# First products taken on x * g with rstd applied later, first loads in order of use on one queue, and w_ada loads moved to that queue

## The chip, the cores and the metric

The kernel runs on one core of one Trainium2 chip. The metric is the device time of one execution in microseconds (us), lower is better. The engines are TensorE (PE; PEld is its weight load), VectorE (DVE), ScalarE (ACT), GpSimd (POOL) and SyncE (SP). Each takes its instructions in order; SP does nothing here but issue DMAs.

## The reference

Two transformer blocks on 256 tokens of width 2048, in float32. What matters here is the beginning of the first block, and the context path and the modulation vectors of the second:

```python
def rms_norm(x, g):
    y = xf * lax.rsqrt(jnp.mean(xf * xf, axis=-1, keepdims=True) + NORM_EPS)
    return (y * g).astype(x.dtype)
def first_block(...):
    h = rms_norm(x, pre_mix_g[l])
    z = h @ w_in[l]                       # q, k, v for chunked attention, u for a pooling branch
    ...
def adaln(cond, w_ada, b_ada):
    return jnp.split(jax.nn.silu(cond) @ w_ada + b_ada, ADA_CHUNKS, axis=-1)
def second_block(...):
    m_lat = [m[:, None, :] for m in adaln(c, w_ada[l], b_ada[l])]
    m_ctx = adaln(c_ctx, w_ada[l], b_ada[l])
    hc = modulate(rms_norm_2(ctx, norm1_g[l]), m_ctx[0], m_ctx[1])
    pc = hc @ w_in_l[:, :KV_WIDTH]
    ...
```

The first block ends with an up and a down projection with a convolution between them (ffn1); the second projects K and V of context and tokens (w2kv), queries and gates, attends, merges (wbr, wout) and has a feed-forward layer of its own.

## The kernel before

All large weights stream through one ring (`Stream`). A *piece* is 128 x 1024 values, 512 KB, loaded by SP into one of four buffers w (L204). `prep` makes of it a rounded part h (ScalarE, L237) and the rest l (VectorE, L238), five buffers each; it may run four pieces ahead of TensorE. A piece is two *slabs* of 512 columns. A slab is used by `token_major` (tokens by outputs, three products per tile: L392, L393, L395) or `feature_major` (outputs by tokens, L359, emptied by `folded`, L367 and L368). After each slab `done` prepares what it can, and adds `pace` to a credit; each full credit runs one `step`.

A step is one product of the modulation (L536): VectorE multiplies a 128 x 1024 tile v of w_ada with a row of the condition that lies broadcast in SBUF (`crow`, L510), and sums it. The tiles, 192 in all, are loaded by GpSimd into two buffers v (L211), each reissued by the step that has read it. The first 64 tiles serve two steps each, the others one. `PACE` holds the steps per slab for feature-major and token-major work; `limit` says up to which tile the steps may go in a stage.

```python
PACE = ((0.2, 0.3), (0.24, 0.36), None, (0.0, 0.3), (0.1, 0.13))   # block1, ffn1, -, wbr and wout, last layer
self.pace = 0.0, (132 - S.vdone) / 80                             # K and V of block 2, at tile 88
```

The limits are 64 and then 88 tiles up to the end of ffn1, 128 in K and V of block 2, 160 in wbr and wout, and 192. In K and V of block 2 a slab is used for four token tiles, and a chunk of 16 slabs fills four of seven PSUM banks, which are emptied at its end.

`Side` holds tasks as Python generators; `tick`, once a slab, lets them emit their next part, and a yield of n waits n ticks. So the order of the instructions on each engine is the order in which this code runs. One such task is `ctx_norm`. It starts in ffn1 when the modulation of the context is known, and goes twice through a tile of the context: it loads each of four parts of 512 columns and squares it (L883, ScalarE L477), forms rstd (L428, and a power on GpSimd, L429), loads each part again (L890), scales it (VectorE, L892), transposes it on TensorE (L452), applies the modulation (L459, L461) and splits it into h and l (L337, L338). The loads go to a ring of two buffers and are issued by GpSimd, as are the w_ada loads.

At the start, x is loaded in pieces of 512 columns, tile 0, then the gain, then weights, then tile 1. Each tile's squares are summed, rstd is formed, x is scaled by rstd and gain (L439), transposed and split. `staged` runs the first eight blocks of 128 inputs for tile 0 alone, then tile 1 is made ready, and the other blocks follow. The result of this first product is half of v; q, k and u follow feature-major.

Of the kernel before, what the change touches and what calls it, by code (L numbers as in the profile page):

```python
# [190 lines left out]
class Stream:  # L191
# [4 lines left out]
    def __init__(self, nc, w, h, l, v, side):  # L196
        self.nc, self.w, self.h, self.l, self.v, self.side = nc, w, h, l, v, side
        self.items, self.vitems, self.steps = [], [], deque()
        self.loaded = self.mains = self.pos = self.retired = self.vloaded = self.vdone = 0
        self.pace, self.credit, self.limit, self.hold = 0.0, 0.0, 0, 0  # L200

    def load(self):
        while self.loaded < len(self.items) and self.loaded < self.mains + len(self.w):
            self.nc.sync.dma_start(self.w[self.loaded % len(self.w)], self.items[self.loaded])  # L204
            self.loaded += 1

    def vload(self):
        while self.vloaded < len(self.vitems) and self.vloaded < self.vdone + len(self.v):
            src, fns = self.vitems[self.vloaded]
            t = self.v[self.vloaded % len(self.v)]  # L210
            self.nc.gpsimd.dma_start(t, src)  # L211
            self.vloaded += 1
            for k, fn in enumerate(fns):
                self.steps.append((fn, t, k == len(fns) - 1))

    def step(self):
        if not self.steps:
            self.vload()
        fn, t, last = self.steps.popleft()
        fn(t)  # L220
        if last:
            self.vdone += 1
            self.vload()

    def finish(self):
        while self.vdone < self.limit:
# [30 lines left out]
    def done(self, ahead=True):  # L257

        self.pos += 1
        self.retired = self.pos // 2  # L260
        if not ahead:
            return
        self.fill()
        self.credit += self.pace
        while self.credit >= 1:
            self.credit -= 1
            if self.vdone < self.limit and self.side.now >= self.hold:
                self.step()


class Kernel:
# [200 lines left out]
    def norm_t(self, *args):  # L472
        for step in self.norm_b(*args):
            step()
# [13 lines left out]
    def constants(self):  # L488
        nc, a = self.nc, self.a
        self.ident = self.g(P)  # L490
        self.ones = self.g(2)
        self.mhalf = self.g(1)
        self.vecs = self.g(NVEC)
        self.ada_v = {n: self.g(16) for n in ("sh1", "sc1", "csh1", "csc1", "sh2", "sc2", "gate")}
        self.g1, self.gc1, self.g2 = self.g(16), self.g(16), self.g(16)
        self.lam, self.ss = self.g(1), self.g(8)
        self.subln = self.g(1)
        self.stats = self.g(128)
        self.sti = 0
        self.junk = self.g(512)  # L500
        self.small = self.g(P)
# [97 lines left out]
    def block1(self):  # L599
        nc, a, side, S = self.nc, self.a, self.side, self.S  # L600
        side.limit, side.per = 1, 1

        xt = self.slot(6, F32).rearrange("p (t d) -> p t d", t=2)
        hx, hh, hl = self.pair(0)
        xr = a["x"].rearrange("(t p) d -> p t d", p=P)
        nc.scalar.copy(self.stats[:, 0:1], self.mhalf)
        grow = self.slot(4, F32)[:, :D]
        for t in range(2):
            for c in range(4):
                nc.sync.dma_start(xt[:, t, c * 512:(c + 1) * 512], xr[:, t, c * 512:(c + 1) * 512])  # L610
            if t == 0:
                nc.sync.dma_start(grow, a["prg"].to_broadcast([P, D]))
                S.load()
        nc.scalar.dma_start(self.vecs, a["vec"])
        self.xs = self.ring(512, 4)

        def start(t):
            ss = self.stat(4)
            for c in range(4):
                self.sumsq(xt[:, t, c * 512:(c + 1) * 512], ss[:, c:c + 1])  # L620
            return self.pre_norm(t, xt, ss, grow)
        self.meet(self.norm_b(start(0), 0, hh, hl))
        xs1 = start(1)
        first = self.token_major([(hh, hl, 0), (hh, hl, 1)], self.staged(lambda: self.norm_t(xs1, 1, hh, hl)))

        _, ah, al = self.pair(2)
        qk = self.slot(4, F32R).rearrange("p (s k t) -> p s k t", s=4, k=4)
# [5 lines left out]
        scr = [s6[:, 2048 + i * 384:2048 + (i + 1) * 384] for i in range(4)]  # L633
        self.gtop = self.gbase + 1024 + 2048
        ut = self.g(8 * 272).rearrange("p (k t) -> p k t", k=8)
        pa, pb = (self.g(544).rearrange("p (k t) -> p k t", k=2) for _ in range(2))
# [57 lines left out]

        def uproj():
            for fb in range(8):
                self.folded(self.feature_major(hx), ut[:, fb, 16:])
                if fb % 2:
                    side.add(pool(fb // 2))

        def qkproj(which):
            z = None
            for j in range(5):
                last, z = z, self.folded(self.feature_major(hx), xq[j % 2]) if j < 4 else None
                if j:
                    self.split(qk[:, 2 * which, j - 1, :], qk[:, 2 * which + 1, j - 1, :], last)

        def mix():
# [19 lines left out]
        def head(h):  # L728

            j = h % 4  # L730
# [3 lines left out]
            bank = self.sb()  # L734
# [4 lines left out]
            sc = 1.0 / math.sqrt(P)  # L739
            mx, sm = self.stat(2), self.stat(2)  # L740
            for q, (lo, hi) in enumerate(((0, P), (P, 384))):
                nc.vector.scalar_tensor_tensor(s[:, lo:hi], bank[:, 2 * lo:2 * lo + hi - lo], sc, tab[:, h, P:] if q == 0 else tab[:, h, :],
                                               op0=ALU.mult, op1=ALU.add)
                nc.vector.reduce_max(mx[:, q:q + 1], s[:, lo:hi], axis=AX, negate=True)
                nc.scalar.activation(s[:, lo:hi], s[:, lo:hi], AF.Exp, bias=mx[:, q:q + 1], accum_out=sm[:, q:q + 1])
# [7 lines left out]
            bank = self.sb()  # L753
# [9 lines left out]
            bank = self.sb()  # L763
# [829 lines left out]
```

## Time and profile before

| | before |
|---|---|
| median of 3 runs | 2799.04 us (2794.86 to 2801.4) |
| the profiled execution | 2798.22 us, span 2796.1 us |
| TensorE busy | 2709.5 us |
| VectorE busy | 2017.0 us |
| ScalarE busy | 1335.9 us |
| GpSimd busy | 254.0 us |

The span runs from the first to the last instruction of the profiled execution; some 2 us of its time lie around it. Busy time leaves out DMA issues and waits. The granted clock, 1 for 2.4 GHz and 0.5 for 1.2 GHz, has a mean of 0.989 over the span.

### The profile page before, as it was taken

The page shows a single profiled execution, that of the slowest core. Times are in us where ns is not written, and L with a number is a line of the kernel's source. Part 1 is how long each engine was busy: PE and PEld are TensorE (multiplying, and loading weights), DVE is VectorE, ACT ScalarE, POOL GpSimd, SP SyncE. Part 2 cuts the span into 40 slices and gives each one's busy share as a digit, 9 for nine tenths or more (in the row PEclk, how much of TensorE's full clock was granted, in tenths as well). Part 3 has the DMA queues.
Part 4 walks back from the last instruction along what each step waited for, and adds up shares of the span by engine and source line. Part 5 has one row for each costly group of instructions (what it writes and reads, how often), then busy time and mean ns, then how long its engine had stood idle before and what let it go on. Part 6 is the DMA issues. An engine that isn't in the chain of part 4 may idle for free.

```text
span 2796.1 us, 36791 instructions
## 1 busy us (share of the span) xinstructions
PE 2709.5 (97%) x13654; PEld 2281.2 (82%) x13654; DVE 2017.0 (72%) x2938; ACT 1335.9 (48%) x1994; POOL 254.0 (9%) x397
## 2 busy tenths in 40 slices
PE   8999899999998799999999999999999999999999
PEld 6888787888877688787877788888878888888887
DVE  6888787888877676746567777768766666665566
ACT  5544454545453455522256665544454444444443
POOL 1121000000001100213111010011100000000000
PEclk9999999999998899999999999999999999999999
DMA  7577567676767675565755544489847776766565
GB/s 283 188 235 270 188 211 256 222 257 227 264 223 249 211 234 171 188 231 177 247 188 173 175 163 153 143 302 327 296 162 235 229 234 227 236 205 190 189 201 168
DMA packets 167860, 609.95 MB, mean 218 GB/s; under 512 B 19504, under 2 KB 19696, under 8 KB 166656
## 3 DMA queue, kind: packets, MB, share of 16 engines
q1 hardware_dynamic: 127728, 461.43, 49.1%
q0 software_dynamic: 39808, 145.92, 15.8%
q8 instruction: 107, 1.75, 0.3%
q14 instruction: 73, 0.60, 0.1%
q10 hardware_dynamic: 144, 0.25, 0.0%
HBM read 592.81 MB, written 14.71 MB: 217 GB/s over the span
## 4 chain that ended last, share of the span: by engine, by line
PE 74%; DVE 6%; issue 4%; ACT 3%; DMA 2%; POOL 1%; ACTq 0%; DVEq 0%; POOLq 0%
PE bank L359 29%; PE bank L392 14%; PE bank L393 14%; PE bank L395 14%; DVE l L238 2%; DMA G<-ctx 1%; ACT h L237 1%; DVE G L536 1%; PE bank L342 1%; PE bank L343 1%; PE bank L344 1%; PE bank L1288 1%; PE bank L452 0%; ACT G L477 0%; ACT G L459 0%
## 5 line engine op out<-in xcount | busy, mean ns | idle before, releaser
L238 DVE TENSOR_TENSOR l<-w,h 128x1024 fp32r<-128x1024 f32 x870 | 1063.0, 1228 | 429.8 <-ACT h L237 418.9
L237 ACT CAST h<-w 128x1024 fp32r<-128x1024 f32 x870 | 908.4, 1051 | 591.8 <-PE bank L393 408.7
L359 PE MATMUL bank<-pair,h 128*128 128x512 f32 x3072 | 847.6, 397 | 11.8 <-ACT h L237 11.8
L359 PEld LDWEIGHTS bank<-pair,h 128*128 128x128 f32 x3072 | 529.4, 190 | 82.4 <-ACT h L237 12.6
L392 PE MATMUL bank<-h,pair 128*128 128x512 f32 x1344 | 535.4, 398 | 11.3 <-DVE slot L1203 5.9
L393 PE MATMUL bank<-h,pair 128*128 128x512 f32 x1344 | 526.9, 392 | 1.4 <-DVE pair L338 0.7
L359 PEld LDWEIGHTS bank<-pair,l 128*128 128x128 f32 x3072 | 472.6, 189 | 66.9 <-DVE l L238 0.4
L359 PE MATMUL bank<-pair,l 128*128 128x256 f32 x3072 | 489.9, 281 | 0.0
L395 PE MATMUL bank<-l,pair 128*128 128x512 f32 x1344 | 413.4, 393 | 6.0 <-DVE l L238 5.9
L536 DVE CUSTOM_DVE_ANT_0 G<-v,G 128x1024 bf16<-128x1024 f32 x256 | 329.3, 1286 | 23.6 <-DMA v<-wada 22.6
L392 PE MATMUL bank<-h,slot 128*128 128x512 f32 x768 | 303.2, 395 | 10.6 <-ACT slot L337 7.2
L392 PEld LDWEIGHTS bank<-h,pair 128*128 128x128 f32 x1344 | 253.9, 189 | 69.6 <-issue 12.9
L395 PEld LDWEIGHTS bank<-l,pair 128*128 128x128 f32 x1344 | 254.0, 189 | 63.1 <-DVE l L238 9.0
L393 PE MATMUL bank<-h,slot 128*128 128x512 f32 x768 | 302.5, 394 | 2.0 <-DVE slot L338 2.0
L393 PEld LDWEIGHTS bank<-h,pair 128*128 128x128 f32 x1344 | 253.9, 189 | 52.8 <-DVE pair L338 2.7
L395 PE MATMUL bank<-l,slot 128*128 128x512 f32 x768 | 240.3, 393 | 0.0
L211 POOL DMA_DIRECT2D v<-wada x192 | 102.1, 532 | 1424.2 <-DVE G L536 1371.2
L367 ACT COPY G<-bank 128x256 f32<-128x256 f32 x192 | 71.4, 372 | 263.9 <-PE bank L359 263.9
L392 PEld LDWEIGHTS bank<-h,slot 128*128 128x128 f32 x768 | 146.3, 191 | 42.2 <-ACT slot L337 8.5
L393 PEld LDWEIGHTS bank<-h,slot 128*128 128x128 f32 x768 | 146.3, 191 | 33.9 <-DVE slot L338 3.4
L395 PEld LDWEIGHTS bank<-l,slot 128*128 128x128 f32 x768 | 145.8, 190 | 30.7
L368 DVE TENSOR_TENSOR G<-bank,G 128x256 f32<-128x256 f32 x192 | 81.1, 422 | 121.9 <-ACT G L367 121.7
(217 smaller groups left out, 1710.0 us busy)
## 6 DMA issues: line engine op xcount, KB each, us to landing
v<-wada POOLq DMA_DIRECT2D x192, 512.0 KB, 4.9
w<-wup SPq DMA_DIRECT2D x176, 512.0 KB, 4.4
w<-wgu SPq DMA_DIRECT2D x176, 512.0 KB, 4.0
w<-wdn SPq DMA_DIRECT2D x88, 512.0 KB, 4.5
w<-wfd SPq DMA_DIRECT2D x88, 512.0 KB, 4.0
w<-w SPq DMA_DIRECT2D x66, 512.0 KB, 4.3
w<-w2g SPq DMA_DIRECT2D x64, 512.0 KB, 3.6
w<-w2kv SPq DMA_DIRECT2D x52, 512.0 KB, 4.2
```

What stands on the lines that cost most here:

```text
L211: self.nc.gpsimd.dma_start(t, src)
L237: self.nc.scalar.copy(h, w)
L238: self.nc.vector.tensor_sub(l, w, h.bitcast(F32))
L342: t.matmul(out, ah, bh, start=start, stop=False)
L343: t.matmul(out, ah, bl, start=False, stop=False)
L359: t.matmul(bank[:, :size], w[:, j * P:(j + 1) * P], x[:, kb, :size], start=s == n == 0, stop=s == 3 and n == 7)
L367: self.nc.scalar.copy(z, bank[:, 256:])
L368: self.nc.vector.tensor_add(out, bank[:, :256], z)
L392: self.nc.tensor.matmul(banks[i], xh, h, start=seen[i] == 1, stop=False)
L393: self.nc.tensor.matmul(banks[i], xl, h, start=False, stop=False)
L395: self.nc.tensor.matmul(banks[i], xh, l, start=False, stop=seen[i] == total[i])
L536: nc.vector.tensor_tensor_reduce(out=self.junk.bitcast(mybir.dt.bfloat16), in0=w, in1=self.adat[:, slot * 1024:(slot + 1) * 1024], scale=1 ...
```

## The change

Three things. First, the first products are taken on x * g: rstd, which is one number per token, is applied to the results. v is multiplied as it leaves PSUM (ScalarE with a scale, VectorE with a scalar), u and k by a row of rstd that goes to DRAM and comes back to all partitions (`rt`), and q through the factor on the scores (`rq`). Second, x, gain and the first weights are loaded by SP in pieces in the order of their use, and the first product takes its 16 blocks once for both tiles, with the products, transposes and splits of the next four blocks emitted between them. Third, w_ada is loaded by SP, and the load that refills a buffer is no longer issued by the step that read it, but by `done` when a count (`vdue`, set to 2 by each step) has run out.

```diff
@@ Stream
-    def load(self):
-        while self.loaded < len(self.items) and self.loaded < self.mains + len(self.w):
+    def load(self, most=None):
+        most = len(self.items) if most is None else most
+        while self.loaded < most and self.loaded < self.mains + len(self.w):
...
-            self.nc.gpsimd.dma_start(t, src)
+            self.nc.sync.dma_start(t, src)
...
         if last:
             self.vdone += 1
-            self.vload()
+            self.vdue = 2
...
         self.fill()
+        self.vdue -= 1
+        if self.vdue == 0:
+            self.vload()
         self.credit += self.pace
...
@@ ada_begin
         self.S.limit, self.S.hold = limit, self.side.now + ROWS
+        if not self.S.steps:
+            self.S.vload()
@@ block1
+        for c in range(4):
+            nc.sync.dma_start(xt[:, 0, cs[c]], xr[:, 0, cs[c]])
+            nc.sync.dma_start(grow[:, cs[c]], a["prg"][:, cs[c]].to_broadcast([P, 512]))
+            if c < 2:
+                S.load(2 * c + 1)
+            nc.sync.dma_start(xt[:, 1, cs[c]], xr[:, 1, cs[c]])
+            if c < 2:
+                S.load(2 * c + 2)
...
+        def scaled(c, t):
+            z, bank = xs(), self.sb()
+            nc.vector.tensor_mul(z, xt[:, t, cs[c]], grow[:, cs[c]])
+            for j in range(4):
+                nc.tensor.transpose(bank[:, j * P:(j + 1) * P], z[:, j * P:(j + 1) * P], self.ident)
+            return bank
...
+        def chunk(c):
+            for t, bank in enumerate([scaled(c, 0), scaled(c, 1)]):
+                parts(c, t, bank)
+                S.prep()
+            squares(c - 1)
...
+        first = self.token_major([(hh, hl, 0), (hh, hl, 1)], [
+            self.seg(range(1), ahead=False, after=lambda: chunk(1)), self.seg(range(1, 5), ahead=False, after=lambda: chunk(2)),
+            self.seg(range(5, 9), ahead=False, after=lambda: chunk(3)), self.seg(range(9, 12), after=lambda: squares(3)),
+            self.seg(range(12, KB))])
+        rrow = self.dpool.tile([1, 256], F32, name="rrow")
         for t in range(2):
...
+            self.rstd(ss[t], D, rr[:, t:t + 1], count=4)
+            nc.gpsimd.dma_start(rrow[:, t * P:(t + 1) * P].rearrange("o p -> p o"), rr[:, t:t + 1])
+        nc.vector.tensor_scalar_mul(rq, rr, 1.0 / math.sqrt(P))
...
+        nc.gpsimd.dma_start(rt, rrow.to_broadcast([P, 256]))
...
-                self.folded(self.feature_major(hx), ut[:, fb, 16:])
+                u = self.folded(self.feature_major(hx), ut[:, fb, 16:])
+                nc.vector.tensor_mul(u, u, rt)
...
+                    if which:
+                        nc.vector.tensor_mul(last, last, rt)
...
-                self.split(vt[:, 0, t, :], vt[:, 1, t, :], banks[t])
+                v, r = vt[:, 0, t, :], rr[:, t:t + 1]
+                nc.scalar.activation(v, banks[t], AF.Identity, scale=r)
+                nc.vector.scalar_tensor_tensor(vt[:, 1, t, :], banks[t], r, v.bitcast(F32), op0=ALU.mult, op1=ALU.subtract)
```

The change shifts later lines: L211, L238, L338, L429, L439 become L212, L239, L342, L433 and L630, and L883, L890 and L510 become L926, L933 and L514. The order of the instructions moves at three places. A row names line, operation, output and input; in brackets stand the engines and DMA counters that it waits for.

GpSimd before, in the stretch of `ctx_norm`, from the broadcasts of the condition to the third load for scaling (L429 is the power of rstd):

```order
L510 DMA G<-crow 128x1024 [waits DVE_49] x2
L211 DMA v_93<-wada 128x1024 [waits DMASW6_49]
L883 DMA G<-ctx 128x512 x2
L883 DMA G<-ctx 128x512 [waits DMASW3_49,Activation_49]
L211 DMA v_92<-wada 128x1024 [waits DMASW7_49,DVE_49]
L883 DMA G<-ctx 128x512 [waits DMASW4_49,Activation_49]
L211 DMA v_93<-wada 128x1024 [waits DMASW2_49,DMASW0_49,DVE_49]
L429 TENSOR_TENSOR G<-G 128x1 [waits DVE_49]
L890 DMA G<-ctx 128x512 [waits DMASW5_49,DMASW1_49,Activation_49]
...
L890 DMA G<-ctx 128x512 [waits DMASW7_49,Activation_49]
...
L890 DMA G<-ctx 128x512 [waits Activation_49]
```

The same place of GpSimd in the change:

```order
L514 DMA G<-crow 128x1024 [waits DMASW3_49,DMASW1_49,DVE_49]
L926 DMA G<-ctx 128x512 [waits DMASW6_49,DMASW4_49]
L926 DMA G<-ctx 128x512 [waits DMASW7_49,DMASW5_49]
L926 DMA G<-ctx 128x512 [waits DMASW4_49,Activation_49]
L926 DMA G<-ctx 128x512 [waits DMASW5_49,Activation_49]
L433 TENSOR_TENSOR G<-G 128x1 [waits DVE_49]
L933 DMA G<-ctx 128x512 [waits DMASW6_49,Activation_49]
L933 DMA G<-ctx 128x512 [waits DMASW7_49,Activation_49]
L933 DMA G<-ctx 128x512 [waits DMASW2_49,DVE_49]
L933 DMA G<-ctx 128x512 [waits DMASW3_49,DVE_49]
```

Between the loads of ctx stood the issues of w_ada, seven of them between the first and the third load for scaling; now nothing stands there but the power. The wait for VectorE of the third and fourth scaling load is that for its own buffer.

SP in the change, in the down projection at the same time, where before only the rows of w stood:

```order
L205 DMA w_80<-wdn 128x1024 [waits DMAHW5_49,DVE_49]
L212 DMA v_93<-wada 128x1024 [waits DMAHW3_49]
L205 DMA w_81<-wdn 128x1024 [waits DMAHW6_49,DVE_49]
L212 DMA v_92<-wada 128x1024 [waits DMAHW0_49]
L205 DMA w_78<-wdn 128x1024 [waits DMAHW7_49,DVE_49]
L205 DMA w_79<-wdn 128x1024 [waits DMAHW1_49,DVE_49]
L212 DMA v_93<-wada 128x1024 [waits DMAHW3_49]
```

The w_ada loads stand behind weight loads that wait for VectorE, and have no wait of their own for it, here and in all 192 rows.

VectorE before, at the start of the program (L426 and L428 form rstd, l_87 is the l part of the first piece, pair_105 holds the split rows):

```order
L426 TENSOR_REDUCE G<-G 128x1 [waits Activation_49]
L428 TENSOR_SCALAR G<-G 128x1 [waits DVE_49]
L439 SCALAR_TENSOR_TENSOR G<-slot_104,G,slot_107 128x512 [waits DMAHW4_49,DMAHW0_49,Pool_49]
L439 SCALAR_TENSOR_TENSOR G<-slot_104,G,slot_107 128x512 [waits DMAHW1_49]
L439 SCALAR_TENSOR_TENSOR G<-slot_104,G,slot_107 128x512 [waits DMAHW2_49]
L439 SCALAR_TENSOR_TENSOR G<-slot_104,G,slot_107 128x512 [waits DMAHW3_49]
L238 TENSOR_TENSOR l_87<-w_78,h_82 128x1024 [waits DMAHW5_49,Activation_49]
L338 TENSOR_TENSOR pair_105<-bank_75,pair_105 128x4x128 [waits Activation_49]
```

VectorE in the change, at the same place:

```order
L630 TENSOR_TENSOR G<-slot_104,slot_106 128x512 [waits DMAHW2_49,DMAHW1_49]
L239 TENSOR_TENSOR l_87<-w_78,h_82 128x1024 [waits DMAHW3_49,Activation_49]
L342 TENSOR_TENSOR pair_105<-bank_75,pair_105 128x4x128 [waits Activation_49]
L630 TENSOR_TENSOR G<-slot_104,slot_106 128x512 [waits DMAHW4_49]
L239 TENSOR_TENSOR l_88<-w_79,h_83 128x1024 [waits DMAHW5_49,Activation_49]
L342 TENSOR_TENSOR pair_105<-bank_76,pair_105 128x4x128 [waits Activation_49]
L630 TENSOR_TENSOR G<-slot_104,slot_106 128x512 [waits DMAHW7_49,DMAHW6_49]
L630 TENSOR_TENSOR G<-slot_104,slot_106 128x512 [waits DMAHW1_49]
```

The first product of x no longer follows a chain through squares and rstd, and waits only for two loads; the second one, of tile 1, stands behind the first l part and the first split.

## Rows read from the trace of the kernel before

**Rows 1.** Busy time of an engine over the whole span, from the page.

```profile
PE 2709.5 (97%) x13654; PEld 2281.2 (82%) x13654; DVE 2017.0 (72%) x2938; ACT 1335.9 (48%) x1994; POOL 254.0 (9%) x397
```

**Rows 2.** Busy time by stretch: its length, PE, PEld, DVE, ACT, POOL, clock, DMA share.

```profile
140.00:205.00 65.00, 63.21 (x346) 54.48 (x344) 57.57 (x79) 31.26 (x46) 13.87 (x12) 1.00 0.70 234
...
820.00:893.00 73.00, 59.61 (x248) 47.87 (x247) 53.27 (x81) 26.46 (x37) 10.12 (x19) 0.89 0.74 255
893.00:975.00 82.00, 63.63 (x317) 54.18 (x316) 52.38 (x85) 35.98 (x66) 9.26 (x17) 0.87 0.58 195
...
1180.00:1325.00 145.00, 140.72 (x606) 115.58 (x606) 87.21 (x129) 32.70 (x38) 35.49 (x48) 0.98 0.58 198
...
1830.00:2050.00 220.00, 218.91 (x993) 180.86 (x991) 162.56 (x199) 89.46 (x104) 24.32 (x46) 1.00 0.81 291
```

**Rows 3.** TensorE's waits: us in total, times, longest.

```profile
PE bank L452 <- DVE G L892: 12.5, 4, 5.0
PE bank L359 <- ACT h L237: 11.8, 3, 5.9
```

**Rows 4.** Waits of the other engines from 820 to 975 us.

```profile
POOL v L211 <- DVE G L536: 110.9, 19, 13.3
ACT G L477 <- DMA G<-ctx: 32.3, 5, 7.8
...
DVE G L892 <- DMA G<-ctx: 11.8, 3, 4.7
```

**Rows 5.** Timeline near 870 us: start, length; in brackets the idle time before and its end.

```profile
849.62 0.69 DVE L338 TENSOR_TENSOR pair<-G,pair 128x512 fp32r<-128x512 f32 x1 [0.69 <-ACT pair L337]
...
865.15 0.53 POOL L211 DMA_DIRECT2D v<-wada  x1 [3.81 <-DVE G L536]
865.67 0.54 POOL L890 DMA_DIRECT2D G<-ctx  x1
...
872.91 0.49 DVE L892 TENSOR_SCALAR G<-G 128x512 f32<-128x512 f32 x1 [4.55 <-DMA G<-ctx]
...
873.45 0.71 PE L452 MATMUL bank<-G 128*128 128x128 f32 x4 [1.94 <-DVE G L892]
```

**Rows 6.** Timeline of the start, up to the first feature-major matmul.

```profile
4.31 0.63 ACT L477 ACTIVATE G<-slot 128x512 f32<-128x512 f32 x1 [2.09 <-DMA slot<-x]
...
8.69 0.57 POOL L429 TENSOR_TENSOR G<-G 128x1 f32<-128x1 f32 x1 [7.30 <-DVE G L428]
9.84 2.74 DVE L439 SCALAR_TENSOR_TENSOR G<-slot,G,slot 128x512 f32<-128x512 f32 x4 [1.30 <-DMA slot<-prg]
...
11.00 1.05 ACT L237 CAST h<-w 128x1024 fp32r<-128x1024 f32 x1 [2.85 <-DMA w<-w]
...
13.87 0.48 PE L392 MATMUL bank<-h,pair 128*128 128x512 f32 x1
...
39.04 0.39 PE L392 MATMUL bank<-h,pair 128*128 128x512 f32 x1
...
40.40 1.07 PE L359 MATMUL bank<-pair,h 128*128 128x512 f32 x4
```

**Rows 7.** DMA issues: count, KB each, median us to landing; whole span, then stretches.

```profile
v<-wada POOLq DMA_DIRECT2D x192, 512.0 KB, 4.9
w<-wup SPq DMA_DIRECT2D x176, 512.0 KB, 4.4
...
v<-wada POOLq DMA_DIRECT2D x25, 512.0 KB, 4.7
...
w<-wbr SPq DMA_DIRECT2D x46, 512.0 KB, 5.4
...
crow<-G POOLq DMA_DIRECT2D x1, 16.0 KB, 3.3
```

**Rows 8.** Groups of instructions: busy us, mean ns of one, idle before.

```profile
L238 DVE TENSOR_TENSOR l<-w,h 128x1024 fp32r<-128x1024 f32 x870 | 1063.0, 1228 | 429.8 <-ACT h L237 418.9
...
L368 DVE TENSOR_TENSOR G<-bank,G 128x256 f32<-128x256 f32 x192 | 81.1, 422 | 121.9 <-ACT G L367 121.7
```

More of the change, by code (lines that the diff above doesn't have):

```diff
@@ L199, in __init__ @@
         self.loaded = self.mains = self.pos = self.retired = self.vloaded = self.vdone = 0
-        self.pace, self.credit, self.limit, self.hold = 0.0, 0.0, 0, 0
-    def load(self):
-        while self.loaded < len(self.items) and self.loaded < self.mains + len(self.w):
+        self.pace, self.credit, self.limit, self.hold, self.vdue = 0.0, 0.0, 0, 0, 0
+    def load(self, most=None):
+        most = len(self.items) if most is None else most
+        while self.loaded < most and self.loaded < self.mains + len(self.w):
             self.nc.sync.dma_start(self.w[self.loaded % len(self.w)], self.items[self.loaded])
@@ L500, in constants @@
         self.junk = self.g(512)
-        self.small = self.g(P)
+        self.small, self.rx = self.g(P), self.g(4)
         make_identity(nc, self.ident)
@@ L605, in block1 @@
         xr = a["x"].rearrange("(t p) d -> p t d", p=P)
-        nc.scalar.copy(self.stats[:, 0:1], self.mhalf)
-        grow = self.slot(4, F32)[:, :D]
-        for t in range(2):
[L609 to L624, printed above, removed]
+        grow = self.slot(4, F32)[:, :D]
+        cs = [slice(c * 512, (c + 1) * 512) for c in range(4)]
@@ new lines, in block1 @@
+        for c in range(4):
[6 more added lines that the diff above has]
+                S.load(2 * c + 2)
+        nc.scalar.dma_start(self.vecs, a["vec"])
+        nc.scalar.copy(self.stats[:, 0:1], self.mhalf)
+        xs = self.ring(512, 4)
@@ new lines, in block1, with parts @@
+        ss = [self.ss[:, :4], self.ss[:, 4:]]
+        rq, rr = self.rx[:, :2], self.rx[:, 2:]
+        def scaled(c, t):
[4 more added lines that the diff above has]
+            return bank
+        def parts(c, t, bank):
+            self.split(*(d[:, 4 * c:4 * c + 4, t * P:(t + 1) * P] for d in (hh, hl)), bank.rearrange("p (k t) -> p k t", k=4))
@@ new lines, in chunk, with squares @@
+        def chunk(c):
[3 more added lines that the diff above has]
+            squares(c - 1)
+        def squares(c):
+            for t in range(2):
+                self.sumsq(xt[:, t, cs[c]], ss[t][:, c:c + 1])
+        begin = [scaled(0, 0)]
+        S.prep()
+        parts(0, 0, begin[0])
+        begin.append(scaled(0, 1))
+        S.prep()
+        parts(0, 1, begin[1])
+        first = self.token_major([(hh, hl, 0), (hh, hl, 1)], [
+            self.seg(range(1), ahead=False, after=lambda: chunk(1)), self.seg(range(1, 5), ahead=False, after=lambda: chunk(2)),
+            self.seg(range(5, 9), ahead=False, after=lambda: chunk(3)), self.seg(range(9, 12), after=lambda: squares(3)),
+            self.seg(range(12, KB))])
@@ L633, in block1 @@
         scr = [s6[:, 2048 + i * 384:2048 + (i + 1) * 384] for i in range(4)]
+        rt = s6[:, 3584:3840]
+        nc.gpsimd.dma_start(rt, rrow.to_broadcast([P, 256]))
         self.gtop = self.gbase + 1024 + 2048
@@ L738, in head @@
             s = scr[j]
-            sc = 1.0 / math.sqrt(P)
             mx, sm = self.stat(2), self.stat(2)
             for q, (lo, hi) in enumerate(((0, P), (P, 384))):
-                nc.vector.scalar_tensor_tensor(s[:, lo:hi], bank[:, 2 * lo:2 * lo + hi - lo], sc, tab[:, h, P:] if q == 0 else tab[:, h, :],
+                nc.vector.scalar_tensor_tensor(s[:, lo:hi], bank[:, 2 * lo:2 * lo + hi - lo], rq[:, q:q + 1], tab[:, h, P:] if q == 0 else tab[:, h, :],
                                                op0=ALU.mult, op1=ALU.add)
```

## The prediction

> **What bounds the kernel now.** I read the busy table first: TensorE is busy for 97% of the span [rows 1], so a change elsewhere can only win what TensorE spends idle or at the lower of its two clock levels. The table of stretches shows where that time lies. From 820 to 975 us TensorE is busy for 59.6 of 73 and 63.6 of 82 us, and the mean granted clock is 0.89 and 0.87 [rows 2]; in the other stretches shown it is busy for 97 to 99.5%. The list of TensorE's waits names the cause's last link: in that stretch it waits 12.5 us for the scaled context rows and 11.8 us for a cast of weights [rows 3]. The waits of the other engines give the link before: ScalarE waits 32.3 us there for loads of ctx to square, VectorE 11.8 us for loads of ctx to scale, and GpSimd spends 110.9 us waiting to issue w_ada loads [rows 4].
>
> The timeline shows how these hang together [rows 5]. The buffer that a ctx load fills was free at 850.3 us, when VectorE's split had read it (849.62 + 0.69). But GpSimd issues in order, and ahead of this load stood four w_ada loads, each waiting until VectorE has read its buffer; the last of them went out at 865.15. So the ctx load went out at 865.67, landed at 872.9, VectorE had sat idle for 4.55 us by then, and TensorE, whose transposes come next in its order, for 1.94. Meanwhile the l parts of later weights stood behind the same VectorE instruction. The pattern repeats for most of the ctx loads.
>
> The other idle time is the start: first main matmul at 13.87 us, first feature-major matmul, which ends the first product, at 40.40 [rows 6].
>
> **The ctx stretch, the largest term.** All 192 w_ada issues leave GpSimd. The ctx loads keep their program order, but now wait only for their own buffers: for the third scaling load that is the split at 850.3, some 15 us earlier than 865.67. A landing of 7.2 us (865.67 to 872.9) is then over by 858, and VectorE came to its scaling near 868 (872.91 less 4.55). The first squares' load stays late: it is issued after the broadcasts of the condition vector, as before. What can be won is TensorE's idle time, 13.4 + 18.4 = 31.8 us, and the clock: a mean of 0.89 and 0.87 between levels of 1 and 0.5 (2.4 and 1.2 GHz) puts 0.22 x 73 + 0.26 x 82 = 37.4 us at the lower one; TensorE was busy for 123.2 of 155 us, so about half of 0.795 x 37.4, that is 14.9 us, is lost. Together 46.7 us: TensorE's own work there is 108 us.
>
> VectorE won't let it have all of this. It works 53.3 + 52.4 = 105.7 us in the stretch [rows 2], almost as long. To that come the bubbles where it waits for ScalarE's half of a split (0.69 us in rows 5, for eight context chunks 5.5 us), and new waits for w_ada: the reload now goes out two slabs after the read, so that in the part with 11 loads at 0.36 a slab the lead falls from 5 or 6 slabs to 3 or 4, that is 4.1 to 5.4 us at 1.36 a slab (40.40 - 39.04 [rows 6]), against a landing of 4.9 [rows 7]: 0 to 0.8 us each, at most 9. VectorE then needs 111 to 120 us. Four prepared pieces, 8 slabs or 11 us, are its lead, but transposes that TensorE reaches in order expose part of any lag. I take a stretch of 121 us: **-34 us**. Bounds: -46.7 if the lead covers everything, and -20 if VectorE's lag is exposed throughout (120 plus another 15 for the clock).
>
> **The start.** The first x piece of 256 KB landed at 4.31, and the first weights, 2.25 MB later on the same queue, at 11.00 [rows 6]: 2.97 us per MB. In the new order the first gain piece lands at 5.05, w0 at 6.5, x of tile 1 at 7.3, w1 at 8.8, the second pieces of x and gain by 10.3, that of tile 1 at 12.5. On VectorE the first product ends near 5.8 (one of the four L439 in 2.74 takes 0.68); then in its order the l part of w0 (after ScalarE's cast, 7.6 + 1.2 = 8.9, L238 [rows 8]), a split (0.68 like the product), and the second product to 10.2. TensorE's first matmul comes near 10.8 instead of 13.87, and block 0 ends near 12.8. From the transposes of chunk 1, near 13.5, TensorE finds all its inputs ready: 15 blocks x 1.36 = 20.4 us, and 24 transposes at about 0.11 = 2.6. The first product ends at 36.5 instead of 40.40: **-4 us**. Bounds: 0, if VectorE's order (8 products, 8 splits, 8 l parts) lags at each chunk, and -6, with the first matmul as early as w0's cast permits.
>
> **What rstd costs now.** Sixteen products by the row of rstd on VectorE, 0.42 us each as the sum of the same size L368 [rows 8]: 6.8 us, most of it between 60 and 205 us, where VectorE is busy for up to 89% [rows 2]; the cover is its idle 11%, and what spills over I put at **+1** (0 to 6.8). The two activations that replace the casts of v, and the scale taken from a column instead of a constant, keep their operand sizes: nothing. Storing rstd as a row and reading it back stands on GpSimd ahead of a memset that VectorE waits for in order: two powers (0.57 each, [rows 6]), three issues (0.53 each, [rows 5]) and a landing of 3.3 us [rows 7] hold VectorE for about 6 us at the end of the first product. Four prepared pieces cover 8 x 1.36 = 10.9 us, and VectorE needs about 9.5 until the fifth is ready, with four small copies, the two operations on v and one l part: nothing, or +3 if a landing is late. The row itself is read 28 us later, by the first k block.
>
> **Weights behind w_ada.** In the order of SP no w_ada load waits for VectorE: the weight load ahead of it already waits for something later. So these 192 issues hold nothing up but the bandwidth. The Trainium skill, in DMA: Bandwidth & Descriptors (Issuing engines are not separate DMA queues), says that issuing engines share the same 16 DMA engines and that spreading DMAs over them saves only issue time; by that rule the move gives and costs no bandwidth, and this term is zero. The same page (Queues, rings and completion order) says that an engine takes turns between queue rows, packet by packet; that speaks against the change, since on one row a weight load behind w_ada waits for all of it. The price from rows: 512 KB at 2.97 us per MB is 1.5 us more, so 5.9 after 4.4, and 6.9 after 5.4 in the stretch from 1830 on [rows 7]. A weight buffer is filled again four pieces ahead, 10.9 us less its cast (1.05, [rows 6]) and l part, so about 8.6. Zero.
>
> **K and V of block 2.** PACE gives (132 - 88)/80 = 0.55 steps a slab here, a step each 1.8 slabs of 2.73 us (twice 1.36: four token tiles). `vdue` is set to 2 by each step, so when two steps fall in adjoining slabs, the reload slips into the slab of its use. By the counts in the code that happens 6 times with no lead and 7 times with one slab: on VectorE 6 x 4.7 [rows 7] + 7 x (4.7 - 2.7) = 42 us. VectorE is busy for 60% there [rows 2], 82 us are free over 205, and a wait of 5 us is far inside a lead of four pieces, here 21.8 us. I take **+0**, with +60 as the other end (below).
>
> **Sum.** -34 - 4 + 1 = -37 on the profiled 2798.2 (0.8 below the median of 2799.0): 2761, and as a median 2762.
>
> **Rivals.** *VectorE becomes the bound of the ctx stretch.* For it: 105.7 us of work against 108, and the new waits. Against it: it enters the stretch with its full lead. Then the stretch gives 10 to 20, and the time is 2775 to 2786. *The loads of ctx stay late*, because their buffers, not GpSimd, hold them: 850.3 against 865.67 speaks against it; only the start is left, 2795. *Weights late behind w_ada*: it decides when landings pass 8.6 us, and the busiest stretch (DMA share 0.81 [rows 2]) is the place; with 9.6 us, the 32 w_ada loads that the limits 128 and 160 let through there cost 1 us each, and the time is 2794. *Slower: the waits for w_ada in block 2's K and V reach TensorE.* The place is the 13 late reloads; it decides when VectorE's lag passes the 21.8 us lead, or falls on an emptying of banks. Then 42 us of idle time, and with it slow clock in the ratio of the ctx stretch (14.9 to 31.8), cost 60: 2822. For it speaks only that one of them stands just ahead of such an emptying.
>
> **How the numbers follow.** Forecast 0.78; VectorE bound 0.11; ctx loads late 0.03; weights late 0.03; slower 0.05. The range of the likeliest, from its bounds, is 2744 to 2780; with the VectorE case it reaches to 2786, and leaves out some 0.15. Within 0.2% (5.6 us, about what a measurement of this kernel can tell from no change) lie the two with 2794 and 2795: 0.06. Faster 0.89, slower 0.05.
>
> **What would show it.** Right: no idle time of ScalarE or VectorE for ctx but the first, the stretch after the context's first load some 30 us shorter at a clock near 1, the first feature-major matmul at 36 to 37. Wrong: TensorE waiting there for l parts (VectorE bound), waits for w_ada on VectorE that TensorE's waits repeat, or ScalarE's casts waiting for weights. The sum fails most easily in how much of VectorE's lag TensorE sees.

## The result, and the profile after

| | before | after |
|---|---|---|
| median of 5 runs | 2798.33 us (2793.25 to 2801.4) | 2783.79 us (2779.05 to 2786.14) |
| ratio | | 0.995 (0.9934 to 0.9966) |
| the profiled execution, its span | 2798.22, 2796.1 us | 2779.05, 2777.3 us |
| VectorE busy | 2017.0 us | 2021.1 us |
| GpSimd busy | 254.0 us | 152.3 us |

The change gains 14.5 us by the medians, where 37 were forecast; the two profiled executions are 19.2 us apart. To see where the forecast went wrong, start times of the same instructions in the two traces are subtracted: a minus means that the changed kernel is ahead there. Lines have their numbers of before: the end of the first product (first L359), the first copies of a head's probabilities (L758), the end of the pooling branch (last L721), a line of the up projection (first L994), K and V of block 2 (first L1203), wbr (first and last L1463), the end (last L359).

| start, us, minus before | first product 40.4 | heads 104.9 | pooling 191.9 | ffn1 568.3 | K, V 1176.1 | wbr 1847.3 | 1947.9 | end 2769.4 |
|---|---|---|---|---|---|---|---|---|
| the change | -2.0 | +5.2 | +6.5 | +8.1 | -22.9 | -23.4 | -18.8 | -19.1 |

So the change first gains 2.0, then loses some 10 up to ffn1, gains 31.0 between 568 and 1176 us, where the context is normed, gains nothing in K and V, and loses 4.6 in wbr.

**The ctx stretch.** Busy time by stretch of the kernel after, in the columns of [rows 2]:

```profile
820.00:893.00 73.00, 66.30 (x307) 54.30 (x306) 60.33 (x93) 33.13 (x52) 3.59 (x7) 0.95 0.77 274
893.00:975.00 82.00, 77.85 (x441) 67.66 (x440) 71.84 (x120) 48.91 (x88) 6.65 (x12) 0.98 0.81 283
...
1830.00:2050.00 220.00, 212.40 (x948) 173.84 (x947) 167.15 (x220) 95.43 (x122) 5.38 (x10) 0.98 0.73 262
```

TensorE is busy for 144.2 us of 155 instead of 123.2, at a clock of 0.95 and 0.98 (the same window holds more of the work than before, 748 TensorE instructions instead of 565; the gain is read from the start times). Its waits from 820 to 975 us (total, times, longest), and with them those of VectorE and ScalarE on loads, answer to [rows 3, 4]:

```profile
PE bank L456 <- DVE G L935: 7.8, 5, 2.7
...
DVE G L542 <- DMA v<-wada: 8.7, 7, 3.4
...
ACT G L481 <- DMA G<-ctx: 2.5, 1, 2.5
```

The waits for ctx are gone but one (over the whole kernel two, 6.9 us, instead of nine); new are VectorE's waits for w_ada. Over the whole kernel they grew from 22.6 us (17 times) to 96.0 (49 times), as the page of after shows in the last column:

```profile
L542 DVE CUSTOM_DVE_ANT_0 G<-v,G 128x1024 bf16<-128x1024 f32 x256 | 329.3, 1286 | 96.9 <-DMA v<-wada 96.0
```

**The first loss, near 50 us.** The timeline of after, GpSimd, then VectorE, TensorE and ScalarE (start, length, in brackets the idle time before and its end):

```profile
42.61 0.58 POOL L660 DMA_DIRECT2D rrow<-G  x1 [0.31 <-DMA w<-w]
50.40 0.55 POOL L672 DMA_DIRECT2D slot<-rrow  x1 [7.21 <-DMA rrow<-G]
50.94 0.23 POOL L684 MEMSET G<- 128x128 f32 x1
...
51.20 0.68 DVE L688 CAST slot<-G 128x128 fp32r<-128x128 f32 x4 [8.69 <-POOL G L684]
51.80 1.40 DVE L816 SCALAR_TENSOR_TENSOR slot<-bank,G,slot 128x512 fp32r<-128x512 f32 x2
...
52.68 1.62 PE L363 MATMUL bank<-pair,h 128*128 128x512 f32 x3 [2.96 <-DVE slot L816]
...
58.15 0.31 ACT L695 ACTIVATE G<-G 32x128 f32<-32x128 f32 x1 [10.72 <-DMA G<-cc]
```

The load of rt waits on GpSimd until rstd has landed in DRAM; the memset behind it waits too, VectorE for the memset for 8.69 us, and TensorE for VectorE. ScalarE waits as well, in the last line: the load of the condition (cc) stands behind the memset and goes out at 52.15 us. Before it went out at 26.21, because the powers of rstd that GpSimd takes ahead of it came at 8.69 and 20.19 us, and now come at 40.11 and 41.73. ScalarE waits 7.8 to 11.1 us for cc in every kernel here with the new start, and never with the old one. No run moves cc by itself, so what this wait costs is open.

**The second, near 110 us**, in the heads: `PE L346` waits 3.52 us for a cast of the probabilities (L799); before it waited 1.0 us there. Both stretches ran at a mean clock of 0.91, against 1.00 in the same windows of before:

```profile
40.00:60.00 20.00, 17.04 (x89) 14.45 (x88) 6.64 (x14) 7.61 (x12) 5.22 (x10) 0.91 0.57 181
100.00:120.00 20.00, 16.29 (x92) 14.21 (x91) 16.66 (x35) 9.31 (x22) 1.09 (x1) 0.91 0.36 128
```

**The third, in wbr.** GpSimd's timeline of after near 1877 us, and VectorE's w_ada steps (only those with a wait):

```profile
1876.88 1.05 POOL L1483 DMA_DIRECT2D slot<-gate  x2 [32.55 <-PE bank L1490]
1877.93 1.08 POOL L874 DMA_DIRECT2D G<-gates  x2
...
1888.00 1.29 DVE L542 CUSTOM_DVE_ANT_0 G<-v,G 128x1024 bf16<-128x1024 f32 x1 [6.24 <-DMA v<-wada]
1892.72 1.28 DVE L542 CUSTOM_DVE_ANT_0 G<-v,G 128x1024 bf16<-128x1024 f32 x1 [1.15 <-DMA v<-wada]
1902.59 1.28 DVE L542 CUSTOM_DVE_ANT_0 G<-v,G 128x1024 bf16<-128x1024 f32 x1 [2.77 <-DMA v<-wada]
```

GpSimd, which no longer has w_ada issues to wait in, sends 1.5 MB of gates at once; then VectorE waits 6.24 us for a w_ada tile, and some 20 us later TensorE 2.7 us for the merged rows (L1490); from 1910 to 1920 us its mean clock is 0.85, where it was 1.00 before.

### The profile page after: what moved, and what is told of

It is laid out like the page before. It is cut to its first block, busy times and chain, and to the rows that moved or that the text cites. A ratio compares the mean times of both kernels' runs of the same rounds, so it can differ in the third digit from the quotient of the medians.

```text
span 2777.3 us, 36672 instructions
## 1 busy us (share of the span) xinstructions
PE 2704.8 (97%) x13654; PEld 2276.7 (82%) x13654; DVE 2021.1 (73%) x2955; ACT 1335.0 (48%) x1994; POOL 152.3 (5%) x208
## 4 chain that ended last, share of the span: by engine, by line
PE 74%; DVE 7%; issue 3%; ACT 3%; DMA 2%; POOL 0%; SPq 0%; ACTq 0%; DVEq 0%; POOLq 0%
PE bank L363 29%; PE bank L396 14%; PE bank L397 14%; PE bank L399 14%; DVE l L239 3%; ACT h L238 1%; DMA v<-wada 1%; DVE G L542 1%; PE bank L346 1%; PE bank L347 1%; PE bank L348 1%; PE bank L1331 1%; DMA G<-ctx 0%; ACT G L481 0%; DVE G L993 0%
## 5 line engine op out<-in xcount | busy, mean ns | idle before, releaser
L239 DVE TENSOR_TENSOR l<-w,h 128x1024 fp32r<-128x1024 f32 x870 | 1060.0, 1225 | 365.4 <-ACT h L238 354.8
L238 ACT CAST h<-w 128x1024 fp32r<-128x1024 f32 x870 | 907.6, 1051 | 593.3 <-PE bank L397 399.3
L1348 ACT ACTIVATE G<-bank,G 128x512 f32<-128x512 f32 x64 | 49.8, 780 | 46.2 <-DVE G L1342 46.0
```

The costliest lines, as they stand in the source:

```text
L238: self.nc.scalar.copy(h, w)
L239: self.nc.vector.tensor_sub(l, w, h.bitcast(F32))
L1348: nc.scalar.activation(d, bank, AF.Exp, bias=mx, scale=rq, accum_out=s)
```

## The experiments

Every run was timed against its own runs of the kernel before (medians 2797.1 to 2797.2). The same subtraction of start times, for one profiled execution of each (it lies up to 4.7 us from the median, so the last column and the medians differ):

| | median us | ratio, interval | 40.4 | 104.9 | 191.9 | 568.3 | 1176.1 | 1847.3 | 1947.9 | 2769.4 |
|---|---|---|---|---|---|---|---|---|---|---|
| e1 | 2769.54 | 0.9900 (0.9886 to 0.9913) | 0.0 | 0.0 | -2.0 | -2.0 | -33.2 | -34.3 | -30.4 | -31.9 |
| e2 | 2815.02 | 1.0062 (1.0050 to 1.0075) | -0.6 | +11.1 | +15.1 | +15.6 | +18.2 | +13.9 | +14.1 | +14.8 |
| e3 | 2779.54 | 0.9939 (0.9926 to 0.9953) | -2.1 | +1.6 | +5.3 | +5.7 | -22.8 | -23.5 | -20.4 | -20.1 |
| e4 | 2766.88 | 0.9898 (0.9883 to 0.9913) | -0.1 | -0.2 | -1.2 | -2.0 | -30.2 | -31.1 | -31.4 | -31.5 |
| e5 | 2772.91 | 0.9914 (0.9900 to 0.9927) | -1.4 | -0.1 | -0.4 | -0.3 | -31.8 | -32.4 | -27.8 | -28.8 |
| e6 | 2777.01 | 0.9932 (0.9920 to 0.9945) | -2.2 | +0.3 | +2.7 | +3.9 | -22.3 | -21.1 | -17.7 | -16.9 |
| e7 | 2767.84 | 0.9901 (0.9888 to 0.9915) | +0.2 | +0.2 | +0.3 | 0.0 | -30.3 | -29.9 | -29.0 | -29.3 |
| e8 | 2783.06 | 0.9950 (0.9937 to 0.9962) | -1.4 | +4.2 | +9.4 | +9.8 | -13.8 | -16.3 | -16.3 | -14.9 |
| e9 | 2759.29 | 0.9866 (0.9852 to 0.9879) | +0.7 | +0.7 | +0.1 | +0.2 | -39.2 | -41.8 | -42.0 | -40.7 |
| e10 | 2786.64 | 0.9962 (0.9949 to 0.9976) | +1.0 | +1.0 | +0.8 | +0.6 | -10.1 | -11.3 | -11.2 | -10.0 |
| e11 | 2769.14 | 0.9900 (0.9890 to 0.9910) | +0.7 | +0.7 | -1.3 | -2.2 | -31.1 | -32.1 | -32.1 | -30.8 |
| e12 | 2774.35 | 0.9928 (0.9914 to 0.9941) | -1.5 | +10.1 | +11.5 | +12.9 | -25.8 | -26.5 | -26.4 | -25.0 |

**e1, the w_ada move alone**, on the kernel before (with the change's other `vdue` lines, as in e4 and e10):

```diff
-            self.nc.gpsimd.dma_start(t, src)
+            self.nc.sync.dma_start(t, src)
...
-            self.vload()
+            self.vdue = 2
```

> The kernel before with the third part of the change alone: w_ada loads on SP, reloaded two slabs late; the start and rstd stay. Theory (the gain comes from GpSimd no longer holding the ctx loads, and the start with rstd applied later is a net loss of some 8 us by 254 us): 2799 - 31 + 5 = about 2772 us, 11 below the changed kernel, with the first feature-major matmul at 40.4 us as before. Rival (the start and the order of first loads give a part of the gain): 2786 or more, slower than the changed kernel.

The theory holds: 27.6 us faster than before, nearly twice the whole change's gain. The first two parts of the change are a loss. The ctx stretch gives 31.2 (-2.0 to -33.2), and wbr takes 3.9 here too, with the old start.

**e2, the first two parts alone** (w_ada on GpSimd, reissued by the step, otherwise the changed kernel):

```diff
-            self.nc.sync.dma_start(t, src)
+            self.nc.gpsimd.dma_start(t, src)
...
-            self.vdue = 2
+            self.vload()
```

> The changed kernel with the w_ada loads as before (on GpSimd, reissued by the step): the first two parts of the change alone. Theory: 8 us slower than the kernel before, some 2806, with the ctx loads late as in the kernel before and TensorE idle there for about 30 us. Rival (the two parts gain, and the changed kernel lost elsewhere): 2797 or less.

Slower, by 17.9 us instead of 8. A part of the rest is one more wait (e12 below has it too, and loses 4.9 there): the first w_ada loads now stand on GpSimd behind the store and load of rstd and the load of cc (54.21 us; before: 26.21), go out at 67.35 us (before: 54.59), and VectorE waits for them. Timeline of e2:

```profile
67.35 1.05 POOL L212 DMA_DIRECT2D v<-wada  x2
...
78.23 1.29 DVE L537 CUSTOM_DVE_ANT_0 G<-v,G 128x1024 bf16<-128x1024 f32 x1 [5.82 <-DMA v<-wada]
```

In the changed kernel SP issues them at 57.34, so the w_ada move makes up there for a loss of the new start.

**e3, rt loaded late**, on the changed kernel:

```diff
-        nc.gpsimd.dma_start(rt, rrow.to_broadcast([P, 256]))
...
             nc.gpsimd.dma_start(cc, a["cc"])
+            nc.gpsimd.dma_start(rt, rrow.to_broadcast([P, 256]))
```

> The changed kernel, with the load of rt (the row of rstd to all partitions) issued on GpSimd behind the memset of ut and the loads of rb, inv and cc instead of ahead of them. Theory (the wait for the stores of rstd on GpSimd holds the memset, that holds VectorE for 8.7 us near 51 us, and TensorE waits and falls to the lower clock): VectorE's wait for the memset is gone, the first head's scores come some 4 us earlier, and the time is 4 to 5 us below the changed kernel, 2779. Rival (VectorE would lag there anyway, by its own work of the fifth prepared piece, the copies and v): less than 1.5 us.

GpSimd's timeline of e3: the memset comes at 43.26, and only the load of rt waits.

```profile
42.68 0.58 POOL L660 DMA_DIRECT2D rrow<-G  x1 [0.30 <-POOL G L433]
43.26 0.23 POOL L683 MEMSET G<- 128x128 f32 x1
...
50.74 0.56 POOL L693 DMA_DIRECT2D slot<-rrow  x1 [5.68 <-DMA rrow<-G]
```

VectorE's wait falls from 8.7 to 0.9 us, TensorE does not wait at 52 us, its clock from 40 to 60 us is 1.00, and the heads' copies come 3.6 us earlier, as expected. The median is 4.2 lower, with intervals that overlap. At the end of this profiled execution 1.0 is left of it: by 192 us the heads have taken back 2.4, and the ctx stretch gives 28.5 here.

**e4, GpSimd kept, two slabs late**, on the kernel before:

```diff
-            self.vload()
+            self.vdue = 2
```

> The kernel before, w_ada still on GpSimd, but reloaded two slabs after the step that has read the buffer. Theory (it is the wait of the w_ada issue for VectorE's read, in GpSimd's order, that holds the ctx loads, and not which queue the bytes are on): most of the stretch's 31 us is gained, 2770 to 2776, and GpSimd's waits of 110.9 us in 820 to 975 us fall below 40. Rival (the two kinds of load must be on different queues): within 8 us of the kernel before.

The time is as the theory had it, 30.3 faster, without the queue being changed. But its reason missed: GpSimd's waits did not fall below 40. Waits of e4 from 820 to 975 us:

```profile
ACT G L480 <- DMA G<-ctx: 15.0, 3, 6.6
...
DVE G L897 <- DMA G<-ctx: 1.2, 2, 0.7
...
POOL v L211 <- DVE G L541: 99.7, 21, 9.2
```

GpSimd still waits 99.7 us for VectorE. What changed is the order: a ctx load now passes ahead of the w_ada issue of the step emitted just before it. I read it as a loop that this opens, which the run does not show by itself: VectorE waits for ctx, its step comes late, so the w_ada issue, so the next ctx load.

**e10, one slab late** (`self.vdue = 1` in e4), to see whether the loop opens by degrees:

> The kernel before, w_ada still on GpSimd, reloaded one slab late instead of two (2766.9 with two). Theory (the ctx load only has to pass ahead of the last w_ada issue, which opens the loop of ctx load, scaling, step, w_ada issue, ctx load; one slab lets some of the twelve ctx loads pass): between, 2772 to 2785. Rival (any delay opens the loop): 2766 to 2769. Rival (what counts is that w_ada comes late, whatever the order): 2780 or more.

The ctx stretch gives 10.7 instead of 28.2 (+0.6 to -10.1), and VectorE waits 7.6 us for ctx between 790 and 975 us, where it waited 11.8 before and 1.2 in e4. That is by degrees, but the median, 2786.64, lies outside the theory's range and within that of the second rival, that only the lateness counts. Against this rival speaks e9, below: there nothing is late, and the gain is the largest.

**e9, the queue alone** (SP, reissued by the step), on the kernel before:

```diff
-            self.nc.gpsimd.dma_start(t, src)
+            self.nc.sync.dma_start(t, src)
```

> The kernel before with w_ada loaded by SP but reissued by the step itself: the queue alone, without the two slabs. Theory (either half alone frees the ctx loads; on SP the issue waits for nothing that the weight load behind it does not wait for): 2767 to 2771, as with the whole w_ada move (2769.5), and VectorE's waits for w_ada stay near the 22.6 us of before. Rival (the two slabs are what counts, since SP now waits for VectorE's step and holds the weights): 2780 or more, with ScalarE's casts waiting for weights.

Better than both theories: 37.8 us faster than before, the fastest kernel here, and its interval lies below those of before, of the change and of e1. The two slabs are no gain on SP but a cost of 10 us. Busy time by stretch, and the waits from 820 to 975 us, of e9:

```profile
820.00:893.00 73.00, 70.15 (x332) 58.38 (x331) 65.45 (x98) 36.06 (x56) 4.86 (x9) 0.95 0.89 311
893.00:975.00 82.00, 79.02 (x448) 68.64 (x447) 72.67 (x122) 50.69 (x86) 4.99 (x9) 1.00 0.79 262
...
PE bank L452 <- DVE G L892: 3.0, 1, 3.0
...
DVE G L536 <- DMA v<-wada: 1.2, 2, 0.8
```

VectorE waits 1.2 us for w_ada instead of the change's 8.7, TensorE 3.0 for scaled rows instead of 7.8. The stretch gives 39.4 (+0.2 to -39.2), and wbr loses nothing. In the seven kernels with w_ada on SP two slabs late (the change, e1, e3, e5, e6, e7, e11) it gives 26.2 to 31.5.

**e12, the same in the changed kernel** (the `vdue` lines undone, SP kept):

```diff
-            self.vdue = 2
+            self.vload()
...
-        if not self.S.steps:
-            self.S.vload()
```

> The changed kernel with the w_ada load reissued by the step itself, on SP: the two slabs undone, the rest of the change kept. Theory (the two slabs cost about 10 us, in the ctx stretch and in wbr, whatever the start does): 2772 to 2776, some 10 below the changed kernel (2783.8), no loss between 1790 and 2010 us, and VectorE's waits for w_ada near 20 us instead of 96. Rival (the two slabs and the start share a loss, so that undoing one gives little): 2780 or more.

As expected: 9.4 lower than the change (the intervals just overlap), 22.9 below before. VectorE's waits for w_ada are 27.7 us, nothing is lost in wbr, and the ctx stretch gives 38.7. It would plausibly be more, had the undoing not also taken the early first load from `ada_begin`: VectorE waits for it once, and the heads start 4.9 us later than in the change. The wait alone does not do it: e9 has one of 5.13 us there, and its heads lose nothing (+0.7, as at 40.4 us). In e12 it follows 8.9 us in which VectorE has waited for the memset. Timeline of e12:

```profile
71.09 1.07 SPq L212 DMA_DIRECT2D v<-wada  x2
...
77.23 1.29 DVE L537 CUSTOM_DVE_ANT_0 G<-v,G 128x1024 bf16<-128x1024 f32 x1 [6.55 <-DMA v<-wada]
```

**e5, no products by rt**, on e3; u and k stay without their factor rstd:

```diff
-                nc.vector.tensor_mul(u, u, rt)
...
-                    if which:
-                        nc.vector.tensor_mul(last, last, rt)
```

> The kernel with the late load of rt (2779.5), without the sixteen products of u and k by rt on VectorE; so it leaves out the scaling of u and k by rstd. Theory (these products, 6.8 us of VectorE's time, delay the heads' softmax, and TensorE waits there for the copies of the probabilities and falls to the lower clock): TensorE's waits between 100 and 120 us fall from 5 us to under 2, the clock there is 1.00, and the time is 4 to 6 us lower, 2774 to 2776. Rival (the heads wait because they now reach the stage with less lead, whatever the products cost): less than 2 us lower, the waits stay.

By the medians 6.6 us lower than e3, and at 192 us 5.7 earlier. From 100 to 120 us, e5, then e3 (busy time by stretch):

```profile
100.00:120.00 20.00, 18.22 (x111) 15.97 (x110) 18.09 (x36) 10.54 (x25) 1.09 (x1) 1.00 0.48 157
```

```profile
100.00:120.00 20.00, 15.81 (x87) 13.72 (x86) 16.73 (x34) 11.98 (x28) 1.09 (x1) 0.91 0.37 126
```

TensorE's waits in these 20 us fall from 4.2 to 1.7, nearly all of them for a head's probabilities, and the clock stays at 1.00.

**e6, these products on GpSimd** (`nc.gpsimd.tensor_mul` in both places of e3):

> The kernel with the late load of rt, with the sixteen products by rt on GpSimd instead of VectorE. Theory (VectorE's time is the cost): as without these products, 2774 to 2777. Rival (the cost is the delay that the product puts into the chain of k, between the sum and its split): no gain, 2779 or more.

Between the theories: 2777.0, at 192 us 2.6 earlier than e3 where e5 was 5.7 (the profiled execution is the slowest of its five, 4.3 above the median). The wait for the probabilities is still 3.5 us, so VectorE's time is one half of the cost and the longer chain plausibly the other; the run does not show the chain by itself.

**e11, SP up to tile 128, GpSimd from wbr on**, both two slabs late:

```diff
+            (self.nc.sync if self.vloaded < 128 else self.nc.gpsimd).dma_start(t, src)
```

> The kernel before with w_ada reloaded two slabs late, on SP for the first 128 tiles and on GpSimd from wbr on. Theory (SP is best in the ctx stretch, 33 us against 29, and GpSimd in wbr and wout, 0 lost against 3 to 4): about 2765, TensorE does not wait for merge_T between 1790 and 2010 us. Rival (the loss in wbr is not from the queue): 2769 or more.

TensorE does not wait for the merged rows and wbr loses nothing (-32.1, -32.1), so the loss there belongs to that queue together with the lateness (e4 and e9 have one of them each, and lose nothing). The median is that of e1 all the same; the ctx stretch gave 28.9 here, 31.2 in e1 and 30.3 in e7, with the same code up to there, so one execution tells it only to some 2 us.

**e7, the late gates on SP**, and half a chunk later, on e1:

```diff
+                (nc.sync if c > 1 else nc.gpsimd).dma_start(mg["g"][c % 2][:, b], gsp[4 * b + c])
...
-            if c < 3:
-                gload(c + 1)
...
+            if c == 0:
+                gload(1)
...
+                self.seg(range(4), after=lambda c=c: gload(c + 1) if 0 < c < 3 else None), self.seg(range(4, 8))])
...
+            g = self.row_chunk(self.gates, c, nc.sync)
```

> The kernel with the w_ada move alone (2769.5), with the gate loads of the third and fourth chunk of wbr, half a chunk later, and the rows of the gates in wout on SP, in line with the weights, instead of GpSimd. Theory (the loss of 3 to 4 us in wbr comes from these 1.5 MB that GpSimd, no longer held by w_ada issues, sends in one burst): VectorE's waits for w_ada between 1790 and 2010 us fall below 12 us from 25, TensorE does not wait there, and the time is 2766 to 2767. Rival (w_ada and the weights on one queue delay each other, burst or not): the waits and the time stay, 2769 or more.

Half right. wbr loses 0.9 instead of 3.9, and TensorE waits only 0.3 us, but VectorE's waits for w_ada stay at 23.9 us: only the longest falls, from 7.0 to 2.5. The burst makes one wait long enough for TensorE to see; the many short ones come with SP and the lateness together (e9, on SP at once, has 3.8 us in the same window; e4, on GpSimd late, 8.9). In the median the two kernels can't be told apart (2767.84, 2769.54).

**e8, all mended**: the changed kernel with e3's and e6's edits and w_ada on GpSimd, two slabs late:

> The changed kernel with w_ada on GpSimd again but reloaded two slabs late, rt loaded late, and the products by rt on GpSimd. Theory (the start's losses are the wait for rt and VectorE's products, so that its 2 us gain at the first product is left; nothing is lost in wbr): 2765, equal to or 2 us below the kernel before with the late reload on GpSimd (2766.9). Rival (the new start is a net loss also with both mended): 2770 or more.

A miss: 9.4 us are lost by 192. The first w_ada loads are again late, at 62.47 us (before: 54.59), and VectorE waits 6.3 us for them once. It is not rt that holds them here, whose load goes out at 51.34, but cc: GpSimd loads it behind the powers of rstd, at 45.15 (before: 26.21), ScalarE waits 8.36 us for it, and the condition's row is stored and broadcast only after that, from 57.08 on. So moving the load of rt and the products does not mend the whole start. wbr loses nothing, as in e4. That the ctx stretch gives 23.6 instead of 28.2 is not explained.

## Why the prediction was wrong

2783.79 lies in the range that was given to the first rival, that VectorE becomes the bound of the ctx stretch. That is chance: the stretch gave 31.0 and not 10 to 20, and the loss came elsewhere.

- **The ctx stretch, -34.** Right: 31.0 in the change. The cause holds too: with the w_ada issues out of GpSimd's order (e9), or behind the ctx loads in it (e4), the loop is open. The two slabs' waits were foreseen at "0 to 0.8 us each, at most 9"; they were 8.7, and the two slabs cost about 8 (e9 gives 39.4, e1 31.2; e12 38.7, the change 31.0).
- **What rstd costs now, +1 and "nothing, or +3 if a landing is late".** This step failed most: by the traces 5.7 at 192 us for the products (e5 against e3, 6.6 by the medians; the upper bound was 6.8) and 3.6 at the heads for the landing, of which 1.2 is left at 192 us and 2.4 at 568. The idle 11% of VectorE was taken as cover. It is no cover where VectorE's order has the product ahead of a head's softmax, for which TensorE waits soon after (4.2 us from 100 to 120 us in e3, 1.7 without the products), at a mean clock of 0.91 instead of 1.00. VectorE's time is only about half of it: on GpSimd the products still cost some 3 us at 192 (e6). The wait for rt held VectorE for 8.69 us instead of about 6, and the four prepared pieces did not cover that: TensorE waited 2.96. The landing was taken from a 16 KB store, 3.3 us [rows 7]; from 38 to 60 us the median is another:

```profile
rrow<-G POOLq DMA_DIRECT2D x2, 0.5 KB, 7.5
```

- **The start, -4.** Mis-sized: -2.0. The first gain piece held VectorE until 6.49 us, not 5.05, the first weights' cast began at 7.82, and the first main matmul came at 12.15, not 10.8; from 14 to 38.4 us TensorE was busy throughout, as foreseen. Timeline of after:

```profile
6.49 0.69 DVE L630 TENSOR_TENSOR G<-slot,slot 128x512 f32<-128x512 f32 x1 [6.49 <-DMA slot<-prg]
...
7.82 1.04 ACT L238 CAST h<-w 128x1024 fp32r<-128x1024 f32 x1 [5.17 <-DMA w<-w]
...
12.15 0.78 PE L396 MATMUL bank<-h,pair 128*128 128x512 f32 x1
```

And the start is worth nothing later: with the products and the wait for rt out of the way (e5), the heads are 0.1 us and the pooling 0.4 us earlier than before. What takes the 2 us back is open; ScalarE's wait for cc, 9.3 us in e5, lies there, and the forecast had no term for it. At 192 us one execution tells no more than some 2 us: e1 and e7 have the same code up to there, and show -2.0 and +0.3.
- **Weights behind w_ada, zero.** Missed by 4.6. The place of the rival was right (wbr), its mechanism wrong: not weights behind w_ada, but w_ada itself, issued late, into a burst of gate loads that GpSimd had held back before. The price of 1.5 us a landing is not there: from 1830 to 2050 us a piece of wbr lands in 5.5 us (median; before 5.8). ScalarE does wait more for weights in wbr (23.4 us from 1790 to 2010, before 9.5), but in e7 it waits 35.1 us for those of wbr and wout, and wbr loses only 0.9. I counted the landings, not what else moves when GpSimd's order is freed. The Trainium skill, in DMA: Bandwidth & Descriptors (Issuing engines are not separate DMA queues), has issuing engines share the same 16 DMA engines; the runs agree that the queue by itself costs no bandwidth here: e9 has all w_ada on SP and loses nothing in wbr (-41.8, -42.0).
- **K and V of block 2, +0.** Right: 0.0 in the change (L1203, first and last, both -22.9). VectorE waited 41.7 us for w_ada between 1100 and 1330 us (8.9 before), against 42 counted; the longest was 5.1 us, inside the lead of 21.8 that the prediction had worked out, and TensorE lost nothing by them.
- **The sum.** Read at 568 us, along e5, e3 and the change: -0.3 for the new start without products and without the wait for rt, +6.0 for the products, +2.4 for the wait for rt, together +8.1; then -31.0 in the ctx stretch, +4.6 in wbr and -0.8 elsewhere: -19.1 at the last line. The split of the +8.1 holds for this order of undoing; the products were not taken out of the change itself. The medians have 14.5; the profiled execution was the fastest of the five.

## What to carry to other kernels

When several loads are issued by one engine in order, ask for each what it waits for: one that waits for a slow reader holds all behind it, and if that reader waits for one of these, the delays feed themselves. Moving such a load to another engine (e9) and issuing it later on the same one (e4) each frees what stood behind it; done together they gain less than the move alone, since the lateness costs 10 us on SP (e1 against e9). Here the move alone (e9, 2759.29 us) beats the kernel before by 37.8 us and the change by some 24. When work is put ahead of others on an engine, look at everything that stands behind it there, loads for a third engine too (cc). And an engine's idle share covers new work only where the order of its instructions puts the idle time ahead of whoever waits.

## What was not expected of the hardware

Two stores of 128 values of 4 bytes each, 0.5 KB from 128 partitions to one row of DRAM, took 7.5 us (median) to land, and 8.2 in e3, while 512 KB of weights took 5.2 in the same stretch. The Trainium skill, in DMA: Bandwidth & Descriptors (Anatomy of one DMA), gives some 2.0 us plus the time for the bytes for a DMA by this path; the trace does not agree for this one, and the measurement decides. The weights beside it do not explain the 7.5 us in the kernel after. The DMA row of the same view has 40 slices of 0.55 us from 38 us on, each with the busy share of the DMA engines in tenths:

```profile
DMA  5989886977400200000000002999569999999998
```

From 44.05 to 51.2 us they are idle but for a little in one slice, and still the load of rt, which waits for the stores, goes out only at 50.40. What passes in these 6 us, the profile does not show.
